# Eight retention states a head updated four at a time, on two halves of the array

## The chip, the cores and the metric

One of the eight cores of one Trainium2 chip runs the whole program: no other core takes part. The metric is the device time of one execution in microseconds (us), the median of the runs. A core has five engines that run side by side and meet at semaphores: TensorE (PE in the profile, its weight loads PEld), VectorE (DVE), ScalarE (ACT), GpSimd (POOL) and SyncE (SP). Here POOL and SP mostly issue DMAs.

## The reference

The reference is one inference step of a two-layer trunk on 336 tokens: 16 meta tokens and 256 prompt tokens, and 8 samples of 8 tokens that carry a state. Only the retention branch matters here, and in it the new states of the samples. For each layer, head and sample:

```python
def retention_chunk(S, q, k, v):
    ...
    scores = jnp.einsum('bihd,bjhd->bhij', q, k) * decay[None]
    intra = jnp.einsum('bhij,bjhe->bihe', scores, v)
    inter = jnp.einsum('bihd,bhde->bihe', q, S) * q_decay[None, :, :, None]
    S_new = S * jnp.exp(n * lg)[None, :, None, None] + jnp.einsum('bjhd,bjhe->bhde', k * k_decay[None, :, :, None], v)
    return S_new, intra + inter
```

A state S is 256 x 256 in float32. There are 2 layers, 8 heads and 8 samples, so 128 states. Each is read from memory, used for `inter`, scaled by a constant of its head, increased by a product of the sample's eight keys and values, and written back.

## The kernel before, in words

All large products run as float32r matmuls on PE, with operands split into a high and a low part (`hi_of` on ACT, `lo_of` on DVE), so that each product is three matmuls: hi by hi, hi by lo, lo by hi. The work is a list of 720 steps. One step is one weight block of 512 KB: `dma_step` loads it from SP some steps ahead (tile `raw`), `split_step` splits it two steps ahead (`whi` on ACT, `wlo` on DVE), and `main_step` issues its 24 matmuls on PE into the tile `acc`. Everything else is an event: `at(s, fn)` puts `fn` behind `main_step(s)` in program order. The order is written out by hand, and each engine works off its own instructions strictly in that order. So an event's matmuls stand in PE's queue between two steps, and PE waits there if their operands are not ready. Events of one step run in the order in which they were registered.

A head of the retention branch takes 16 steps: four each for k, v, q and the gate rg. `head(h)` (from L302) registers its events with `E(d, fn)`, d steps from the head's first. Events with d of 16 and over run during the next head. Those that matter, with their d:

- `turn` transposes k and v into tokens with DVE's 32 x 32 transposes (L333), in four parts; v's last part is at 12.
- `tok` (L159, L165) splits the 128-token blocks of k and v: the high part by ACT, the low part by DVE. Block 2 holds the samples' tokens. For v, blocks 2 and 0 are at 13 and block 1 at 14.
- `stack_out` writes block 2 of the split k or v to a scratch in DRAM from POOL (`ktd`, `vtd`), and `stack_in` reads it back from SP so that the 32 rows of a sample (eight tokens, four combinations of high and low parts) stand on 32 partitions. For k this is the tile `kts`, 128 partitions by 2 groups of four samples. For v it is `vbd`, block-diagonal: four slots of 256 columns a group, of which sample j fills only slot j on its own 32 partitions, and the rest stays zero.
- `ev_q` at 11 rotates q on DVE (four operations, L307 to L310). `split_q` at 12 makes `qhi` (ACT) and `qlo` (DVE), and copies the samples' columns to `qpad` (POOL). `scores2` at 14 multiplies them with k on PE: first khi by qhi, then khi by qlo, and so on.
- `inter` at 15 multiplies `qpad` with the states, in 32 matmuls of 32 stationary columns; `inter_copy` at 16 takes the result.
- `sdo(b)` at 17 + b updates one state: two matmuls of 128 rows by 256 columns (the rows of the other three samples meet zeros), one DVE operation over 512 columns (L444) and one DMA out from POOL (L445). `sload(b)` at 6 + b is the load of one state.
- `pstate`, the prompt's new state, is at 18; `pv` and `norm2` at 17 to 25; `back` at 26 transposes the head's result on PE (L511), and DVE takes it (L513).

In the first head of layer 0 (`kl = 3`) k's events are three steps later, and all four parts of v's `turn` are at 12. PSUM tiles of the events come from a ring of four (`side`).

Of the kernel before, what the change touches and what calls it, by code (L numbers as in the profile page):

```python
# [6 lines left out]
F32 = mybir.dt.float32  # L7
F32R = mybir.dt.float32r
ACTF = mybir.ActivationFunctionType
ALU = mybir.AluOpType  # L10
# [7 lines left out]
NB = 8  # L18
# [3 lines left out]
HD = 256  # L22
# [55 lines left out]
def build(tc, a, o, g8):  # L78
    nc = tc.nc
# [6 lines left out]
    def at(s, fn, *args):  # L86
        events[s].append(lambda: fn(*args))

    def job(wsrc, nk, rhs, c0, evac, lag=0):
        first = len(steps)  # L90
        st = dict(acc=None)
        for j in range(nk):
            steps.append((st, wsrc(j), rhs, 4 * j, c0, j == 0, j == nk - 1))
        last = first + nk - 1
        at(last + lag, lambda: evac(st["acc"]))
        return first, last

    def wblk(w, c):
        return lambda j: w[c // 256, j].rearrange("p (k n) -> p k n", k=4)
# [3 lines left out]
    def open_pool(name, side=None, **kw):  # L103
        P[name] = tc.alloc_tile_pool(name=name, bufs=1, side=side, reuse_waits="tile", **kw)
        return P[name]
# [15 lines left out]
    def side():  # L121
        return sidep.tile([128, 512], F32, tag="side", bufs=4, name="side")
# [31 lines left out]
    def mm(out, lhsT, rhs, start, stop):  # L154
        nc.tensor.matmul(out, lhsT, rhs, start=start, stop=stop)  # L155
# [105 lines left out]
    H = {}  # L261

    for l in range(DEPTH):
# [13 lines left out]
        def open_r(l=l, a_side=a_side):  # L277
            p = open_pool("r", side=a_side)
            t = p.tile([128, 2, 8, 32], F32, name="qpad")
            nc.gpsimd.memset(t, 0.0)  # L280
            H["qpad"] = t
            for key in ("kr", "vr"):
                t = p.tile([128, 2, 384], F32, name=key)
                nc.gpsimd.memset(t[:, :, T:384], 0.0)
                H[key] = t
            t = p.tile([128, SC], F32, name="sc")
            nc.gpsimd.memset(t[64:128, NR0 + NR1:SC], 0.0)
            H["sc"] = t
            t = p.tile([128, 2, 4, HD], F32R, name="vbd")
            nc.gpsimd.memset(t.bitcast(F32), 0.0)  # L290
            H["vbd"] = t
            for key in ("kt", "vt"):
                t = p.tile([128, HD], F32R, name=key + "tail")
                nc.gpsimd.memset(t[64:128].bitcast(F32), 0.0)
                H[key + "tail"] = t
# [4 lines left out]
        def head(h, l=l, c0=c0, n=n, nt=nt):  # L300
            hs = {}
            rp = lambda shape, dt, tag, bufs=1: P["r"].tile(shape, dt, tag=tag, bufs=bufs, name=tag)  # L302
# [47 lines left out]
            def stack_in(key):  # L350
                rows = hs[key + "d"].rearrange("g c t e -> (g c t) e")
                nc.sync.dma_start(out=H[key + "tail"][0:64].bitcast(F32), in_=rows[0:64])
                src = rows[64:320].rearrange("(f r) e -> r f e", f=2)
                if key == "kt":
                    st = hs["kts"] = rp([128, 2, HD], F32R, "kts")
                    nc.sync.dma_start(out=st.bitcast(F32), in_=src)
                else:
                    for j in range(4):
                        r = slice(32 * j, 32 * j + 32)
                        nc.sync.dma_start(out=H["vbd"][r, :, j].bitcast(F32), in_=src[r])  # L360

            def pstate():
                ps = side()
# [56 lines left out]
                lo_of(plo[:, w], sc[:, w], phi[:, w])  # L420
                hs["p"] = phi, plo

            def sload(b):
                s = rp([128, 2, HD], F32, "sraw", 8)
                nc.sync.dma_start(out=s, in_=a["state_ret"][l, b, h].rearrange("p (d e) -> p d e", d=2))
                hs["s", b] = s

            def inter():
                ps = hs["inter"] = side()
# [4 lines left out]
                            mm(ps[32 * j:32 * j + 32, :HD], H["qpad"][:, d, b], hs["s", b][:, d],  # L434
                               i == 0 and d == 0, i == 1 and d == 1)

            def sdo(b):
                up = side()
                for d in range(2):
                    mm(up[:, HD * d:HD * d + HD], hs["kts"][:, b // 4, 128 * d:128 * d + 128],  # L440
                       H["vbd"][:, b // 4, b % 4], True, True)
                s = hs.pop(("s", b))
                s2 = s.rearrange("p d e -> p (d e)")
                nc.vector.scalar_tensor_tensor(out=s2, in0=s2, scalar=g8[h], in1=up, op0=ALU.mult, op1=ALU.add)  # L444
                nc.gpsimd.dma_start(out=o["ret_s"][l, b, h].rearrange("p (d e) -> p d e", d=2), in_=s)  # L445

            def ev_rg(acc):
                z, th = tmp(), tmp()
# [69 lines left out]
            b0, e = job(wblk(w_in, OFF["k"] + HD * h), 4, h_rhs, 0, ev_k, 3 if l == 0 and h == 0 else 0)  # L518
# [3 lines left out]
            E = lambda d, fn, *ar: at(b0 + d, lambda: fn(*ar))  # L522
# [7 lines left out]
            E(9 + kl, tok, 0, "k", kd(0))  # L530
            E(10 + kl, tok, 1, "k", kd(1))
            E(11 + kl, stack_in, "kt")
            E(13, tok, 2, "v", None)
            E(13, stack_out, "vt")
            E(13, tok, 0, "v", None)
            E(14, tok, 1, "v", None)
            E(15, stack_in, "vt")
            E(12, split_q)
            E(18, pstate)
            E(11, scores)  # L540
            E(14, scores2)
            for b in range(NB):
                E(6 + b, sload, b)
            E(15, inter)
            for b in range(NB):
                E(17 + b, sdo, b)
            E(16, inter_copy)
            E(17, pv, 0)
            E(18, norm2, 0)
            E(19, pv, 1)  # L550
            E(20, norm2, 1)
            E(24, pv, 2)
            E(25, norm2, 2)
            E(26, back)
# [3 lines left out]
        if l == 0:  # L558
            at(6, open_r)
        else:  # L560
            at(r0 - 1, open_r)
        for h in range(HEADS):
            head(h)
# [272 lines left out]
        if l == 0:  # L836
            e = len(steps) - 1
# [87 lines left out]
    for j, (ps, (t0, rows)) in enumerate(zip(sums, YBLOCKS)):  # L925
        nc.vector.tensor_scalar(out=trs[:rows, j:j + 1], in0=ps[:rows, 0:1], scalar1=1.0 / DM, scalar2=EPS,
                                op0=ALU.mult, op1=ALU.add)
# [67 lines left out]
```

## Time and profile before

| | |
|---|---|
| Median of 3 runs (all runs) | 2817.84 us (2817.78, 2817.84, 2819.44) |
| Profiled execution: its time | 2819.04 us |
| Profiled execution: span from first to last instruction | 2816.9 us |
| PE busy | 2800.1 us (99%), 19042 matmuls |
| DVE busy | 1684.9 us (60%) |
| ACT busy | 940.2 us (33%) |
| POOL busy | 291.9 us (10%) |
| Granted PE clock, mean | 0.997 |
| DMA | 516.64 MB, mean 183 GB/s |

The span is what the profile sees; 2.1 us of the execution's time lie around it. Busy PE time is modelled: matmuls overlap one another, so the time that a matmul takes away from the others is read from the distance between two starts, not from its duration. In a timeline the columns are the start in us, the duration in us, engine, line, operation, tile written and tiles read, shape and count, and in brackets the idle time before it and what ended that. An acc row is a matmul of a step, a side row is one of an event.

### The profile page before, as it was taken

The page shows a single profiled execution, that of the slowest core. Times are in us where ns is not written, and L with a number is a line of the kernel's source. Part 1 is how long each engine was busy: PE and PEld are TensorE (multiplying, and loading weights), DVE is VectorE, ACT ScalarE, POOL GpSimd, SP SyncE. Part 2 cuts the span into 40 slices and gives each one's busy share as a digit, 9 for nine tenths or more (in the row PEclk, how much of TensorE's full clock was granted, in tenths as well). Part 3 has the DMA queues.
Part 4 walks back from the last instruction along what each step waited for, and adds up shares of the span by engine and source line. Part 5 has one row for each costly group of instructions (what it writes and reads, how often), then busy time and mean ns, then how long its engine had stood idle before and what let it go on. Part 6 is the DMA issues. An engine that isn't in the chain of part 4 may idle for free.

```text
span 2816.9 us, 46574 instructions
## 1 busy us (share of the span) xinstructions
PE 2800.1 (99%) x19042; PEld 2778.0 (99%) x19042; DVE 1684.9 (60%) x2418; ACT 940.2 (33%) x1121; POOL 291.9 (10%) x547
## 2 busy tenths in 40 slices
PE   9999999999999999999999999999999999999998
PEld 9999999999999999999999999999999999999998
DVE  8777777744345664344467777777543455644543
ACT  5333333333233333233333333333332333333333
POOL 1211111110000000000112212211100000000001
PEclk9999999999999999999999999999999999999999
DMA  6666665655544444444546666666555454444443
GB/s 228 227 211 212 212 212 207 216 200 170 166 163 149 147 148 135 155 167 163 188 167 218 219 225 225 215 213 212 207 182 173 161 166 148 145 158 164 173 163 129
DMA packets 174262, 516.64 MB, mean 183 GB/s; under 512 B 23888, under 2 KB 46672, under 8 KB 174032
## 3 DMA queue, kind: packets, MB, share of 16 engines
q1 hardware_dynamic: 151264, 448.37, 46.6%
q0 software_dynamic: 21696, 63.99, 6.4%
q8 instruction: 149, 2.44, 0.4%
q10 hardware_dynamic: 1088, 1.31, 0.1%
q14 instruction: 65, 0.53, 0.1%
HBM read 447.91 MB, written 66.57 MB: 183 GB/s over the span
## 4 chain that ended last, share of the span: by engine, by line
PE 99%; DVE 1%; DMA 0%; issue 0%; POOL 0%; SPq 0%; DVEq 0%; ACT 0%; ACTq 0%
PE acc L155 93%; PE side L155 6%; PE side L511 0%; DVE tok L333 0%; DMA raw<-in_w_in_dram 0%; DVE xf L937 0%; DVE wlo L165 0%; PE side L252 0%; POOL trs L928 0%; DVE qlo L165 0%; DVE tmp L307 0%; DVE tmp L308 0%; DVE whi L190 0%; DVEq L983 0%; DVE xs L809 0%
## 5 line engine op out<-in xcount | busy, mean ns | idle before, releaser
L155 PE MATMUL acc<-act_hi,whi 128*128 128x320 f32 (+1 forms) x3328 | 1038.0, 312 | 0.0
L155 PE MATMUL acc<-act_lo,whi 128*128 128x320 f32 (+1 forms) x3328 | 1037.5, 312 | 0.0
L155 PE MATMUL acc<-act_hi,wlo 128*128 128x320 f32 (+1 forms) x3328 | 1036.1, 311 | 0.0
L165 DVE TENSOR_TENSOR wlo<-raw,whi 128x1024 fp32r<-128x1024 f32 (+1 forms) x721 | 866.1, 1219 | 262.4 <-ACT whi L159 251.7
L159 ACT CAST whi<-raw 128x1024 fp32r<-128x1024 f32 x719 | 736.6, 1046 | 619.3 <-PE acc L155 445.6
L155 PE MATMUL acc<-h_hi,whi 128*128 128x336 f32 x2304 | 731.0, 319 | 0.0
L155 PE MATMUL acc<-h_lo,whi 128*128 128x336 f32 x2304 | 728.2, 318 | 1.1 <-DVE h_lo L167 1.1
L155 PE MATMUL acc<-h_hi,wlo 128*128 128x336 f32 x2304 | 726.2, 317 | 0.0
L155 PEld LDWEIGHTS acc<-act_hi,whi 128*128 128x128 f32 x3328 | 624.8, 188 | 3.3 <-ACT tmp L450 3.3
L155 PEld LDWEIGHTS acc<-act_lo,whi 128*128 128x128 f32 x3328 | 626.4, 188 | 0.0
L155 PEld LDWEIGHTS acc<-act_hi,wlo 128*128 128x128 f32 x3328 | 625.2, 188 | 0.0
L155 PEld LDWEIGHTS acc<-h_lo,whi 128*128 128x128 f32 x2304 | 435.8, 190 | 1.5 <-DVE h_lo L167 1.5
L155 PEld LDWEIGHTS acc<-h_hi,whi 128*128 128x128 f32 x2304 | 432.5, 188 | 3.6 <-ACT tmp L450 3.3
L155 PEld LDWEIGHTS acc<-h_hi,wlo 128*128 128x128 f32 x2304 | 433.2, 188 | 0.0
L444 DVE SCALAR_TENSOR_TENSOR sraw<-sraw,side 128x512 f32<-128x512 f32 x128 | 87.7, 685 | 185.3 <-PE side L155 185.3
L445 POOL DMA_DIRECT2D out_ret_s_dram<-sraw x128 | 70.7, 552 | 566.4 <-DVE sraw L444 560.7
L333 DVE STREAM_TRANSPOSE tok<-vr 32x192 f32<-32x192 f32 (+1 forms) x256 | 90.3, 353 | 4.3
L333 DVE STREAM_TRANSPOSE tok<-kr 32x192 f32<-32x192 f32 (+1 forms) x256 | 90.3, 353 | 4.1
L611 DVE SCALAR_TENSOR_TENSOR mb<-tr,acc 128x336 f32<-128x336 f32 (+1 forms) x32 | 14.4, 492 | 81.0 <-PE acc L155 81.0
L775 DVE SCALAR_TENSOR_TENSOR mt<-tp,acc 128x336 f32<-128x336 f32 (+1 forms) x32 | 14.4, 492 | 80.4 <-PE acc L155 80.4
L809 DVE SCALAR_TENSOR_TENSOR xs<-acc,xo 128x672 f32<-128x672 f32 (+2 forms) x17 | 13.5, 800 | 80.5 <-PE acc L155 80.5
L275 DVE TENSOR_TENSOR tp<-acc,rstd 128x672 f32<-128x672 f32 (+1 forms) x16 | 13.5, 841 | 80.4 <-PE acc L155 80.4
(170 smaller groups left out, 1756.1 us busy)
## 6 DMA issues: line engine op xcount, KB each, us to landing
raw<-in_w_in_dram SPq DMA_DIRECT2D x512, 512.0 KB, 4.3
sraw<-in_state_ret_dram SPq DMA_DIRECT2D x128, 256.0 KB, 4.7
out_ret_s_dram<-sraw POOLq DMA_DIRECT2D x128, 256.0 KB, 3.5
raw<-in_proj_ret_dram SPq DMA_DIRECT2D x64, 512.0 KB, 4.1
raw<-in_proj_pool_dram SPq DMA_DIRECT2D x64, 512.0 KB, 4.9
raw<-in_w_out_dram SPq DMA_DIRECT2D x64, 512.0 KB, 4.7
raw<-in_pool_w_dram SPq DMA_DIRECT2D x16, 512.0 KB, 3.3
kts<-ktd SPq DMA_DIRECT2D x16, 256.0 KB, 3.2
```

The source lines that it names most:

```text
L155: nc.tensor.matmul(out, lhsT, rhs, start=start, stop=stop)
L159: nc.scalar.copy(out=out, in_=in_)
L165: nc.vector.tensor_tensor(out=out, in0=in_, in1=hi.bitcast(F32), op=ALU.subtract)
L275: nc.vector.tensor_tensor(out=tile_[:, :, n], in0=acc[:, :, n], in1=bc(rstd[:, n]), op=ALU.mult)
L333: nc.vector.transpose(dst[32 * t:32 * t + 32, :, 0:nb, a_], src[q, :, 0:nb, t])
L444: nc.vector.scalar_tensor_tensor(out=s2, in0=s2, scalar=g8[h], in1=up, op0=ALU.mult, op1=ALU.add)
L445: nc.gpsimd.dma_start(out=o["ret_s"][l, b, h].rearrange("p (d e) -> p d e", d=2), in_=s)
L611: nc.vector.scalar_tensor_tensor(out=t[:, d, n], in0=H["tr", l, i][:, d, n], scalar=1.0, in1=acc[:, d, n], op0=ALU.add, op1=ALU.mult)
L775: nc.vector.scalar_tensor_tensor(out=t[:, d, n], in0=H["tp", l, i][:, d, n], scalar=1.0, in1=acc[:, d, n], op0=ALU.add, op1=ALU.mult)
L809: nc.vector.scalar_tensor_tensor(out=xs[:, p, n], in0=acc[:, p, n], scalar=0.5, in1=xo[:, p, n], op0=ALU.mult, op1=ALU.add)
```

## The change

The states are held, loaded and written in pairs. `sload(p)` loads samples 2p and 2p + 1 with one DMA, at 6 + 2p. `vbd` keeps two slots instead of four: sample j goes to slot j mod 2, so that a group's partitions 0 to 63 hold samples 0 and 1 as a block diagonal, and 64 to 127 samples 2 and 3. `update(g)` replaces four calls of `sdo`: for each half d of the state's rows and each half r of the partitions, one matmul of 64 rows by 512 columns into a PSUM tile of its own, then four DVE operations of 512 columns, then two DMAs out. The two halves r use different rows of the array and different PSUM tiles. The events are moved too: v's `tok` of block 2 and `stack_out` from 13 to 12, ahead of `split_q`; `stack_in` of v from 15 to 14; `scores2` from 14 to 13; `inter` from 15 to 14; `inter_copy` from 16 to 15; the updates from 17 to 24 to 16 and 18; `pv` 0 and 1 to 20 and 21; `pstate` from 18 to 23.

```diff
-            t = p.tile([128, 2, 4, HD], F32R, name="vbd")
+            t = p.tile([128, 2, 2, HD], F32R, name="vbd")
...
-                        nc.sync.dma_start(out=H["vbd"][r, :, j].bitcast(F32), in_=src[r])
+                        nc.sync.dma_start(out=H["vbd"][r, :, j % 2].bitcast(F32), in_=src[r])
...
-            def sload(b):
-                s = rp([128, 2, HD], F32, "sraw", 8)
-                nc.sync.dma_start(out=s, in_=a["state_ret"][l, b, h].rearrange("p (d e) -> p d e", d=2))
-                hs["s", b] = s
+            def sload(p):
+                s = rp([128, 2, 2, HD], F32, "sraw", 4)
+                nc.sync.dma_start(out=s, in_=a["state_ret"][l, 2 * p:2 * p + 2, h].rearrange("b p (d e) -> p b d e", d=2))
+                for b in range(2):
+                    hs["s", 2 * p + b] = s[:, b]
+                hs["pair", p] = s
...
-            def sdo(b):
-                up = side()
-                for d in range(2):
-                    mm(up[:, HD * d:HD * d + HD], hs["kts"][:, b // 4, 128 * d:128 * d + 128],
-                       H["vbd"][:, b // 4, b % 4], True, True)
-                s = hs.pop(("s", b))
-                s2 = s.rearrange("p d e -> p (d e)")
-                nc.vector.scalar_tensor_tensor(out=s2, in0=s2, scalar=g8[h], in1=up, op0=ALU.mult, op1=ALU.add)
-                nc.gpsimd.dma_start(out=o["ret_s"][l, b, h].rearrange("p (d e) -> p d e", d=2), in_=s)
+            def update(g):
+                ups = [(d, r, side()) for d in range(2) for r in range(2)]
+                for d, r, up in ups:
+                    rows = slice(64 * r, 64 * r + 64)
+                    mm(up, hs["kts"][rows, g, 128 * d:128 * d + 128],
+                       H["vbd"][rows, g].rearrange("p j e -> p (j e)"), True, True)
+                for d, r, up in ups:
+                    s = hs["pair", 2 * g + r]
+                    nc.vector.scalar_tensor_tensor(out=s[:, :, d], in0=s[:, :, d], scalar=g8[h],
+                                                   in1=up.rearrange("p (j e) -> p j e", j=2), op0=ALU.mult, op1=ALU.add)
+                for r in range(2):
+                    p = 2 * g + r
+                    nc.gpsimd.dma_start(out=o["ret_s"][l, 2 * p:2 * p + 2, h].rearrange("b p (d e) -> p b d e", d=2),
+                                        in_=hs["pair", p])
...
-            E(13, tok, 2, "v", None)
-            E(13, stack_out, "vt")
+            E(12, tok, 2, "v", None)
+            E(12, stack_out, "vt")
             E(13, tok, 0, "v", None)
             E(14, tok, 1, "v", None)
-            E(15, stack_in, "vt")
+            E(14, stack_in, "vt")
             E(12, split_q)
-            E(18, pstate)
             E(11, scores)
-            E(14, scores2)
-            for b in range(NB):
-                E(6 + b, sload, b)
-            E(15, inter)
-            for b in range(NB):
-                E(17 + b, sdo, b)
-            E(16, inter_copy)
-            E(17, pv, 0)
-            E(18, norm2, 0)
-            E(19, pv, 1)
-            E(20, norm2, 1)
+            E(13, scores2)
+            for p in range(4):
+                E(6 + 2 * p, sload, p)
+            E(14, inter)
+            E(15, inter_copy)
+            E(16, update, 0)
+            E(18, update, 1)
+            E(20, pv, 0)
+            E(21, norm2, 0)
+            E(21, pv, 1)
+            E(22, norm2, 1)
+            E(23, pstate)
             E(24, pv, 2)
             E(25, norm2, 2)
             E(26, back)
```

## Rows read from the trace of the kernel before

**Rows 1.** The page: busy time and share, and the chain that ended last.

```profile
PE 2800.1 (99%) x19042; PEld 2778.0 (99%) x19042; DVE 1684.9 (60%) x2418; ACT 940.2 (33%) x1121; POOL 291.9 (10%) x547
PE 99%; DVE 1%; DMA 0%; issue 0%; POOL 0%; SPq 0%; DVEq 0%; ACT 0%; ACTq 0%
```

**Rows 2.** The page's costliest groups: count | busy us, mean ns of one | idle before.

```profile
L444 DVE SCALAR_TENSOR_TENSOR sraw<-sraw,side 128x512 f32<-128x512 f32 x128 | 87.7, 685 | 185.3 <-PE side L155 185.3
L445 POOL DMA_DIRECT2D out_ret_s_dram<-sraw x128 | 70.7, 552 | 566.4 <-DVE sraw L444 560.7
```

**Rows 3.** Timeline of PE: two states' updates and what starts behind each.

```profile
302.80 0.40 PE L155 MATMUL side<-vbd,kts 128*128 128x256 f32 x2
303.03 0.28 PE L155 MATMUL side<-vthi,phi 128*128 128x256 f32 x1
...
307.45 0.40 PE L155 MATMUL side<-vbd,kts 128*128 128x256 f32 x2
307.69 0.32 PE L155 MATMUL acc<-h_hi,whi 128*128 128x336 f32 x1
```

**Rows 4.** Timeline of PE around one inter; its second row is of a shorter stretch.

```profile
353.13 0.31 PE L155 MATMUL acc<-h_hi,wlo 128*128 128x336 f32 x1
353.37 0.42 PE L155 MATMUL side<-sraw,qpad 128*32 128x256 f32 x4
353.37 1.93 PE L155 MATMUL side<-sraw,qpad 128*32 128x256 f32 x32
355.23 0.42 PE L155 MATMUL acc<-h_hi,whi 128*128 128x336 f32 x1
355.49 0.31 PE L155 MATMUL acc<-h_lo,whi 128*128 128x336 f32 x1
```

**Rows 5.** Timeline of DVE in the fifth head of layer 0.

```profile
332.71 1.04 DVE L513 SCALAR_TENSOR_TENSOR tmp<-side,vec,sg 128x336 f32<-128x336 f32 x2 [0.46 <-PE side L511]
343.66 0.86 DVE L165 TENSOR_TENSOR qlo<-tmp,qhi 128x672 fp32r<-128x672 f32 x1
```

**Rows 6.** Timeline of ACT in the same head.

```profile
339.41 0.76 ACT L159 CAST qhi<-tmp 128x672 fp32r<-128x672 f32 x1 [6.06 <-DVE tmp L310]
343.32 0.74 ACT L159 CAST vthi<-tok 80x256 fp32r<-80x256 f32 x2 [2.21 <-DVE tok L333]
```

**Rows 7.** Timeline of PE in the same head: first matmuls of step 14 and of scores2.

```profile
343.99 0.32 PE L155 MATMUL acc<-h_hi,whi 128*128 128x336 f32 x1
347.71 0.29 PE L155 MATMUL side<-qhi,khi 128*128 128x272 f32 x1
```

**Rows 8.** Timeline of DVE in the second head of layer 1.

```profile
1543.48 1.01 DVE L513 SCALAR_TENSOR_TENSOR tmp<-side,vec,sg 128x320 f32<-128x320 f32 x2
1554.29 0.83 DVE L165 TENSOR_TENSOR qlo<-tmp,qhi 128x640 fp32r<-128x640 f32 x1
```

**Rows 9.** Timeline of ACT in the second head of layer 1.

```profile
1553.96 0.75 ACT L159 CAST vthi<-tok 80x256 fp32r<-80x256 f32 x2 [2.23 <-DVE tok L333]
```

**Rows 10.** Timeline of PE there: first matmuls of step 14 and of scores2.

```profile
1554.13 0.31 PE L155 MATMUL acc<-act_hi,whi 128*128 128x320 f32 x1
1557.63 0.28 PE L155 MATMUL side<-qhi,khi 128*128 128x256 f32 x1
```

**Rows 11.** Timeline of PE in the first head of layer 0: scores2.

```profile
64.75 0.29 PE L155 MATMUL side<-qhi,khi 128*128 128x272 f32 x1
66.64 0.39 PE L155 MATMUL side<-qlo,khi 128*128 128x272 f32 x1 [1.60 <-DVE qlo L165]
```

**Rows 12.** Timelines of ACT and DVE in that head.

```profile
64.60 0.74 ACT L159 CAST vthi<-tok 80x256 fp32r<-80x256 f32 x2 [4.12 <-DVE tok L333]
64.93 0.88 DVE L167 SCALAR_TENSOR_TENSOR ktlo<-tok,cst,kthi 80x256 fp32r<-80x256 f32 x2
65.73 0.85 DVE L165 TENSOR_TENSOR qlo<-tmp,qhi 128x672 fp32r<-128x672 f32 x1
```

**Rows 13.** Busy time by stretch: engines' us, then the granted clock, DMA share, GB/s.

```profile
67.90:71.20 3.30, 3.30 (x17) 3.30 (x16) 3.00 (x7) 0.26 (x1) 3.30 (x5) 0.50 0.27 66
```

## The prediction

> **What bounds the kernel now.** I read the page first. PE is busy for 99% of the span, and the chain that ended last is 99% PE [rows 1]. So what counts is PE's time: matmuls that are taken off it are worth what they occupy, and a wait that the change puts into PE's queue costs its full length. DVE, ACT, POOL, SP and the DMAs cost something only where PE comes to wait for them. Next I read the timelines of PE around the updates, for what they occupy, and around `inter`, the one place where this kernel already splits the array. Last I read DVE, ACT and PE together from `back` to `scores2`, because the change moves `scores2` one step forward.
>
> **What the updates occupy now.** There are 128 states, each with one operation on L444 and one DMA on L445 [rows 2], and two matmuls for each. What a pair takes from PE is the distance of starts: 302.80 to 303.03 and 307.45 to 307.69, 0.23 and 0.24 us, so some 0.118 a matmul [rows 3]. The updates occupy 256 x 0.118 = 30.2 us. The change makes 32 batches, each in place of eight matmuls, 0.94 us.
>
> **What they will occupy.** A matmul of 512 columns should take twice one of 256, 0.236 us. If the two halves stream at once, a batch streams for 2 x 0.236 = 0.47 us; if they don't, for 4 x 0.236 = 0.94. No row shows matmuls of 64 rows. The nearest is `inter`, which splits the array by columns: four of its matmuls start within 0.04 us of one another, and 32 of them take 353.37 to 355.23, 0.058 us each, half of what a full-array matmul of as many columns takes, though each is a slower f32 pass [rows 3, 4]. So parts of the array do work at once here, and I take the halves to do so.
>
> The same rows price the passage from whole array to parts and back. A step's matmuls follow each other in 3.72 / 24 = 0.155 us [rows 7]. The last one ahead of `inter` is followed after 0.24 (0.085 too much). From there to the next step's first matmul it is 1.86 us; the groups of four follow each other in (1.93 - 0.42) / 7 = 0.216, eight of them are 1.73, and the other 0.13 is passage; and the first matmul behind it occupies 0.26, 0.105 too much, because its weights could not be loaded ahead [rows 4]. Together 0.32 us [rows 4]. A half of the array gets 128 columns of weights where `inter` gets 32; I add 0.08 for that, from the 0.105 that 128 exposed columns cost, and take 0.40 a batch. So a batch is 0.47 + 0.40 = 0.87 us and 32 are 27.9: **2 us gained**. With no price for the passage it is 15.1 us and the gain 15.1; with the passage and no overlap it is 32 x 1.34 = 42.9 us and a loss of 13. I take the 2, since the passage of `inter` is the nearest row, and keep both ends.
>
> The Trainium skill has this as a rule against the change: by its page TensorEngine Tiling (Array Packing), Key Properties, a switch of the tiling mode drains the array. The 0.32 us around `inter` agree for columns; no row shows it for halves of rows. By the rule the gain is the 2 us, without it the 15.
>
> **The step that decides: scores2 one step earlier.** DVE's line from `back` to `qlo` is fixed. At `back` DVE waits for PE (0.46 us idle ahead of L513), and from there to `qlo` it has no idle time worth a row: 332.71 to 343.66 [rows 5]. In layer 1 the same line runs from 1543.48 to 1554.29 [rows 8]. None of the work that the change takes off DVE lies in these steps (`back` is d = 10, `qlo` d = 12 of the next head; the evacuations were at d = 1 to 8 and will be at 0 and 2). The line's start is tied to PE's transposes, so a lighter DVE before that doesn't pull it forward.
>
> PE reaches `scores2` now at 347.71, one step behind 343.99 [rows 7]; it will reach it at 343.99, and its second matmul, the one that reads `qlo`, would be due at 344.12. Now `qlo` ends at 344.52 [rows 5]: already 0.4 late. And the change puts v's `tok` of block 2 ahead of `split_q` in step 12. On ACT the high part of v, which waits for v's last transposes until 343.32, now stands in front of `qhi`, which today ran at 339.41 [rows 6]. So `qhi` starts at 343.32 + 0.34 (two such casts take 0.74) = 343.66 and ends 0.76 later at 344.42; `qlo` needs it, takes 0.86 and ends at 345.30; PE sees that 0.05 later (66.58 to 66.64 in the first head [rows 11, 12]), at 345.35. **The wait is 345.35 - 344.12 = 1.23 us**, in seven heads of layer 0. In layer 1: v's high part at 1553.96, `qhi` (0.73, as 640 of 672 columns of 0.76) 1554.30 to 1555.03, `qlo` to 1555.88, PE at 1555.93, due at 1554.13 + 0.13 = 1554.26: **1.67 us**, in eight heads [rows 8 to 10].
>
> In the first head of layer 0 PE waits already, 1.76 us from 64.88 to 66.64 [rows 11]. There all of v's transposes are in step 12, and v's low part (0.40, as one of the two ktlo) now stands ahead of `qlo`: 65.73 + 0.40 + 0.85 + 0.05 = 67.03 [rows 12]. PE is due at 64.75 - 3.72 + 0.13 = 61.16. The wait becomes 5.87 us, 4.1 more.
>
> Sum: 7 x 1.23 + 8 x 1.67 + 4.1 = **26.1 us lost**. The lower bound has `qhi` untouched and `qlo` later by v's low part alone (0.40): 0.85 and 1.31 us a head, 7 x 0.85 + 8 x 1.31 + 4.1 = 20.5. I take 26.1: the order in ACT's queue is plain in the diff.
>
> **The clock.** Behind the 1.76 us wait of the first head the granted clock was 0.50 from 67.90 to 71.20 [rows 13], the lower of the two levels (1.2 of 2.4 GHz): half of 3.3 us, some 1.65 us, were lost again. The new waits are 1.23 and 1.67 us, with one matmul in between; whether they cost the clock too no row says. I count none beyond the first head's, which has its loss already; the other end is 15 x 1.65 = 25 us.
>
> **Edits that I cost at nothing.** DVE's evacuations: the same number, 8 of 0.69 us a head [rows 2], over as many elements, now in two bursts of 2.7 us behind steps 16 and 18, where DVE has one split of weights a step and little else; if that cover failed, `wlo` of two steps later would be late by what is over. The four PSUM tiles of a batch: the last of them is `inter`'s, which `inter_copy` must have read. It comes behind the gate's work: one operation of 672 columns on DVE (as `qlo`, 0.86), one on ACT (as `qhi`, 0.76), two of 336 on DVE (as L513, 1.04), then the copy's low part (as ktlo, 0.4), 3.1 us in all [rows 5, 6, 12]. The batch starts a step behind the gate's last matmul, 3.5 to 3.7 us, its fourth matmul later still. If the copy were late, that matmul alone would wait, some tenths. The states' loads: the same bytes, pair 3 issued at 12 and read at 14, now with PE's wait in between. v's way through DRAM: each link one step earlier, the distances between them as now; but `qpad`'s copies on POOL now queue behind four DMA issues, two of which wait for v's low part (343.7 + 0.4). With 0.55 us an issue [rows 2] the copies begin near 346; PE reads `qpad` in `inter`, a step behind `scores2`, past 349. `pv`, `norm2` and `pstate` move in the queue and occupy what they did; k's and v's tiles are written again only at d = 9 to 14 of the next head. 64 fewer DMA issues each on SP and POOL relieve queues that bound nothing.
>
> **The sum.** 26.1 - 2.3 (30.2 - 27.9) = 23.8 us more. The profiled execution took 2819.04 us, 2816.9 of them span; it would take 2842.8. The median of the runs is 1.2 lower: 2817.84 + 23.8 = **2841.6 us**.
>
> **The rivals.**
> - *The halves cost no passage.* For it: `inter`'s cost could be that of column parts. The gain is 15.1: 2817.84 + 26.1 - 15.1 = 2828.8. Chance 0.17.
> - *The clock falls at the waits.* For it: the first head's 1.76 us did it; against: the others are shorter. If all eight of layer 1 do, 8 x 1.65 = 13 us: 2855; if all 15, 2866. Chance 0.14.
> - *The halves stream one after the other.* For it: no row shows rows split. 42.9 - 30.2 + 26.1 = 38.8: 2856.6. Chance 0.06.
> - *Faster after all: the batches stream freely and the waits are short.* The place is DVE's line from L513 to `qlo`. Were it shorter by some 0.7 us a head, because it starts earlier than PE's transposes let it now or ACT takes `qhi` first, the waits would fall below 15.1 us in all, 0.94 a head; that is the point from which it decides. With waits of 8 us: 2817.84 - 15.1 + 8 = 2811. For it: layer 1's L513 shows no idle time in its row; against: the line needs 10.8 us and has three steps, 10.5 to 11.2. Chance 0.14; another 0.07 lies around no change, with waits of 11 to 20 us.
>
> **How the numbers follow.** The forecast, 2841.6, has 0.42; with the unknowns of its own terms 2833 to 2850. For 8 in 10 the range takes in the free passage with the lower wait (2817.84 + 20.5 - 15.1 = 2823), most of what lies around no change and, above, the serial halves and the clock falling in most heads: **2818 to 2864**. A measurement of this kernel tells 0.2%, 5.6 us, from no change. Faster: 0.14. Within 0.2% (2812.2 to 2823.5): 0.07. Slower, the forecast and the first three rivals: 0.79.
>
> **What would show it.** Right: PE rows of `scores2` with an idle time ended by DVE `qlo` in all 16 heads, 0.7 to 1.7 us each, and 5 to 6 us in the first; ACT's `qhi` directly behind the first `vthi`; two vbd matmuls of 512 columns that start together, 0.8 to 0.9 us from the step's last matmul to where the next would have been. Wrong: no idle time at `scores2`, or pairs of vbd matmuls 0.24 us apart.

## The result, and the profile after

The changed kernel takes 2847.1 us (median; 2845.75 to 2848.62), the kernel before, on the same chip, 2818.4: a ratio of 1.0101 with a 95% interval of 1.0089 to 1.0113. It is 28.7 us slower; the forecast was 23.8 slower, at 2841.6. The profiled execution has a span of 2845.5 us, 28.6 more than before. The page now shows PE on 92% of the chain that ended last, where it was 99% [rows 1], with DVE in between:

```profile
span 2845.5 us, 45976 instructions
PE 2809.9 (99%) x18914; PEld 2761.7 (97%) x18914; DVE 1685.7 (59%) x2418; ACT 936.6 (33%) x1121; POOL 277.3 (10%) x483
PE 92%; DVE 5%; issue 1%; ACT 0%; DMA 0%; POOL 0%; SPq 0%; DVEq 0%; ACTq 0%
L447 DVE SCALAR_TENSOR_TENSOR sraw<-sraw,side 128x512 f32<-128x512 f32 x128 | 79.3, 682 | 56.1 <-PE side L155 56.1
L451 POOL DMA_DIRECT2D out_ret_s_dram<-sraw x64 | 46.2, 726 | 362.7 <-DVE sraw L447 344.7
```

DVE does the same 128 operations of 0.68 us and POOL half as many DMA issues [rows 2]. PE's busy share says little: a step's matmul is given 0.31 us where the next could follow after 0.155, so a part of each wait counts as busy. The view of who waited for whom tells it. For PE its first two rows (us in total, times, longest) are these:

```profile
PE side L155 <- ACT qhi L159: 12.1, 16, 4.5
PE side L155 <- DVE qlo L165: 8.0, 16, 0.7
```

Sixteen heads, sixteen waits for each: all at `scores2`. Before there was one, of 1.6 us [rows 11]. In the timelines of the fifth head of layer 0 the line from `back` to `qlo` is the one of [rows 5 to 7], but for v's split, which now stands ahead of q's on ACT (`vthi` ahead of `qhi`) and on DVE (`vtlo` ahead of `qlo`). PE with one weight load, then ACT, then DVE:

```profile
353.09 0.31 PE L155 MATMUL acc<-h_hi,wlo 128*128 128x336 f32 x1
353.68 0.39 PE L155 MATMUL side<-qhi,khi 128*128 128x272 f32 x1 [0.27 <-ACT qhi L159]
354.57 0.39 PE L155 MATMUL side<-qlo,khi 128*128 128x272 f32 x1 [0.50 <-DVE qlo L165]
354.80 0.29 PE L155 MATMUL side<-qhi,klo 128*128 128x272 f32 x1
...
354.57 0.19 PEld L155 LDWEIGHTS side<-qlo,khi 128*128 128x128 f32 x1 [0.71 <-DVE qlo L165]
...
352.56 0.41 ACT L159 CAST vthi<-tok 80x256 fp32r<-80x256 f32 x1 [9.95 <-DVE tok L333]
352.88 0.75 ACT L159 CAST qhi<-tmp 128x672 fp32r<-128x672 f32 x1
...
341.96 1.04 DVE L520 SCALAR_TENSOR_TENSOR tmp<-side,vec,sg 128x336 f32<-128x336 f32 x2 [0.46 <-PE side L518]
...
348.13 0.50 DVE L310 TENSOR_TENSOR tmp<-tmp 128x336 f32<-128x336 f32 x1
...
351.39 1.48 DVE L333 STREAM_TRANSPOSE tok<-vr 32x192 f32<-32x192 f32 x4
353.00 0.42 DVE L165 TENSOR_TENSOR vtlo<-tok,vthi 80x256 fp32r<-80x256 f32 x1
353.65 0.86 DVE L165 TENSOR_TENSOR qlo<-tmp,qhi 128x672 fp32r<-128x672 f32 x1 [0.23 <-ACT qhi L159]
```

ACT now stands idle for 9.95 us, until v's last transposes are done; for the last 3.9 of them `qhi`, behind the instruction that waits, could have run, since its operand is done at 348.63 (L310). From 353.09 the first matmul of `scores2` would start 0.155 later; it starts after 0.59. The second should follow after 0.125 and follows after 0.89. The third still comes 0.105 late: the second's weights were loaded only with it, both at 354.57, and not ahead of it. Together 0.435 + 0.765 + 0.105 = 1.3 us. In layer 1:

```profile
1569.12 0.30 PE L155 MATMUL acc<-act_hi,wlo 128*128 128x320 f32 x1
1570.15 0.38 PE L155 MATMUL side<-qhi,khi 128*128 128x256 f32 x1 [0.74 <-ACT qhi L159]
1571.01 0.39 PE L155 MATMUL side<-qlo,khi 128*128 128x256 f32 x1 [0.47 <-DVE qlo L165]
1571.23 0.28 PE L155 MATMUL side<-qhi,klo 128*128 128x256 f32 x1
```

That is 0.88 + 0.74 + 0.10 = 1.73 us (1.5 in the first head of layer 1, which has no `back` ahead of it). In the first head of layer 0:

```profile
60.95 0.31 PE L155 MATMUL acc<-h_hi,wlo 128*128 128x336 f32 x1
65.78 0.59 PE L155 MATMUL side<-qhi,khi 128*128 128x272 f32 x1 [4.52 <-ACT qhi L159]
67.04 0.59 PE L155 MATMUL side<-qlo,khi 128*128 128x272 f32 x1 [0.67 <-DVE qlo L165]
```

4.68 + 1.13 = 5.8 us, 4.05 more than the 1.76 before. A batch of the new updates:

```profile
227.46 0.31 PE L155 MATMUL acc<-h_hi,wlo 128*128 128x336 f32 x1
227.70 0.73 PE L155 MATMUL side<-vbd,kts 64*128 64x512 f32 x4
228.36 0.42 PE L155 MATMUL acc<-h_hi,whi 128*128 128x336 f32 x1
228.62 0.32 PE L155 MATMUL acc<-h_lo,whi 128*128 128x336 f32 x1
```

From 227.46 to 228.62 it is 1.16 us, of which two ordinary distances are 0.31: a batch takes 0.85, where eight matmuls took 0.94. And the granted clock, by stretch:

```profile
64.70:74.80 10.10, 8.35 (x34) 8.05 (x35) 7.47 (x14) 5.49 (x9) 4.00 (x10) 0.50 0.40 114
1921.50:1924.80 3.30, 3.30 (x14) 3.30 (x14) 2.35 (x4) 2.57 (x4) 0.07 (x1) 0.50 0.07 24
1925.00:1928.00 3.00, 3.00 (x39) 2.23 (x41) 1.50 (x3) 0.02 (x1) 0.00 (x0) 1.00 0.57 149
```

It is 0.50 over 10.1 us in the first head, where before it was so over 3.3 [rows 13], and once more behind one of the 15 other waits, that of the seventh head of layer 1. PE worked from 67.04 to 74.8 of the first stretch, so 3.9 us were lost there (1.65 before), and 1.65 in the second: 3.9 more than before.

The account: waits 7 x 1.3 + 1.5 + 7 x 1.73 + 4.05 = 26.8; clock 3.9; batches 32 x (0.85 - 0.94) = -2.9. Sum 27.8 of 28.6 us. Compared step by step, by the distances between the first matmuls of the 720 steps, all of the difference lies in the two retention stages, 13.6 and 14.3 us, and none in the stages behind them; 0.7 us of the span lies ahead of the first step and behind the last.

### The profile page after: what moved, and what is told of

Its sections match the earlier page's. It is cut to its first block, busy times and chain, and to the rows that moved or that the text cites. A ratio compares the mean times of both kernels' runs of the same rounds, so it can differ in the third digit from the quotient of the medians.

```text
span 2845.5 us, 45976 instructions
## 1 busy us (share of the span) xinstructions
PE 2809.9 (99%) x18914; PEld 2761.7 (97%) x18914; DVE 1685.7 (59%) x2418; ACT 936.6 (33%) x1121; POOL 277.3 (10%) x483
## 4 chain that ended last, share of the span: by engine, by line
PE 92%; DVE 5%; issue 1%; ACT 0%; DMA 0%; POOL 0%; SPq 0%; DVEq 0%; ACTq 0%
PE acc L155 87%; PE side L155 5%; DVE tok L333 2%; DVE wlo L165 1%; DVE tmp L520 1%; DVE qlo L165 0%; DVE tmp L307 0%; DVE tmp L308 0%; ACT qhi L159 0%; DVE tmp L310 0%; DVE ktlo L167 0%; PE side L518 0%; DMA raw<-in_w_in_dram 0%; DVE xf L944 0%; PE side L252 0%
## 5 line engine op out<-in xcount | busy, mean ns | idle before, releaser
L447 DVE SCALAR_TENSOR_TENSOR sraw<-sraw,side 128x512 f32<-128x512 f32 x128 | 79.3, 682 | 56.1 <-PE side L155 56.1
L451 POOL DMA_DIRECT2D out_ret_s_dram<-sraw x64 | 46.2, 726 | 362.7 <-DVE sraw L447 344.7
L159 ACT CAST vthi<-tok 128x256 fp32r<-128x256 f32 (+1 forms) x48 | 19.3, 403 | 153.1 <-DVE tok L333 153.1
```

The source lines that it names most:

```text
L159: nc.scalar.copy(out=out, in_=in_)
L447: nc.vector.scalar_tensor_tensor(out=s[:, :, d], in0=s[:, :, d], scalar=g8[h], in1=up.rearrange("p (j e) -> p j e", j=2), op0=ALU.mult, op ...
L451: nc.gpsimd.dma_start(out=o["ret_s"][l, 2 * p:2 * p + 2, h].rearrange("b p (d e) -> p b d e", d=2), in_=hs["pair", p])
```

## The experiments

The theory at this point: the loss is PE's wait at `scores2`, because `scores2` came one step forward and `qhi` went behind v's high part in ACT's queue; the batches alone are a small gain. Its rival: the batches, their passage and DVE's bursts are what costs. All ratios are to the kernel before, timed in the same series.

**Moving scores2 back alone** (a_scores14, from the changed kernel).

```diff
-            E(13, scores2)
+            E(14, scores2)
```

> The changed kernel with one event moved back: scores2 at 14 instead of 13. Theory (the loss is PE's wait at scores2 for qlo): the wait is gone in 15 heads; the first head of layer 0 keeps one of about 2.2 us (1.8 before, v's low part of 0.4 now ahead of qlo). The batches keep their gain of 3.1 us, as the trace of the changed kernel has it (a batch 0.85 us, eight matmuls before 0.94). 2818.4 - 3.1 + 0.4 = 2815.7 us. Rival (the batches and DVE's bursts are what costs): the time stays at 2845 to 2847.

Measured: 2818.1 us, ratio 1.000 (0.9991 to 1.0010). So 29.0 us, the whole loss, hang on that step, and the rival falls. It is 2.4 us above the theory's number, and the trace shows both parts. In the first head `inter` now stands directly behind `scores2`, and `qpad`'s copies on POOL, behind the DMA issues of v's scratch, are late:

```profile
70.01 3.64 PE L155 MATMUL side<-sraw,qpad 128*32 128x256 f32 x32 [0.82 <-POOL qpad L393]
67.70:74.40 6.70, 5.88 (x45) 3.55 (x45) 4.73 (x8) 2.05 (x4) 2.66 (x6) 0.50 0.51 144
```

0.8 us of wait, and the clock at half for 6.7 us instead of 3.3: another 1.7.

**Putting split_q ahead of v's split** (b_qfirst, from the changed kernel), with `scores2` still at 13: what belongs to v's split, now ahead of q's, and what to DVE's line?

```diff
+            E(12, split_q)
             E(12, tok, 2, "v", None)
...
-            E(12, split_q)
```

> The changed kernel with split_q registered ahead of v's tok of block 2 in step 12, so that qhi no longer queues behind v's high part on ACT; scores2 stays at 13. Theory: the wait shrinks to what DVE's line alone gives, 0.45 us in seven heads, 0.91 in eight, about 5.4 in the first, each with some 0.13 behind it for the weight load that could not be pulled ahead: 16 us more than before, 3.1 less for the batches, 2 for the clock in the first head: about 2833 us. Rival (DVE's line alone makes the wait, ACT's order is no matter): unchanged, 2847. Rival (ACT's order alone): 2818 or less.

Measured: 2834.8 us, ratio 1.0057 (1.0042 to 1.0072), against 2833 expected. The order of the two splits is worth 12.4 of the 28.7 us; the other 16.4, net of the batches' gain, are DVE's line, which isn't done in time even with `qhi` early. PE's waits are now for `qlo` alone, and none for `qhi`; in the fifth head the second matmul follows the first after 0.59 instead of 0.125, a wait of 0.46 (0.45 expected):

```profile
PE side L155 <- DVE qlo L165: 13.3, 16, 5.3
...
351.42 0.29 PE L155 MATMUL side<-qhi,khi 128*128 128x272 f32 x1
352.01 0.39 PE L155 MATMUL side<-qlo,khi 128*128 128x272 f32 x1 [0.30 <-DVE qlo L165]
```

The 12.4 us are not ACT's queue alone, as the expectation puts it. The edit also takes v's low part from ahead of `qlo` on DVE. In the changed kernel's fifth head it is 0.78 us from the end of v's last transposes (352.87) to the start of `qlo` (353.65); v's low part takes 0.42 of that, and the wait for `qhi` behind it only 0.23. So with ACT's order alone put right, some 0.23 us a head would come back, an estimate from these rows; no run parts the two.

**Putting split_q ahead of v's transposes too** (c_qtop, from the changed kernel): the event is registered before the loop that registers `turn`.

```diff
             E(4 + kl, split_k)
+            E(12, split_q)
...
-            E(12, split_q)
```

> The changed kernel with split_q registered first of all in step 12, ahead of v's last transposes too (ahead of all four parts of them in the first head); scores2 stays at 13. Theory: qlo ends some 1.5 us earlier than in the kernel before and is there when PE comes, in all heads, the first too: no wait at scores2 and no fall of the clock behind it. 2818.4 - 3.1 (batches) - 1.9 (the first head's wait) - 1.7 (its clock) = 2811.7 us. Rival (scores2 at 13 is too early whatever stands ahead of it, or the batches cost): 2820 to 2847.

Measured: 2813.6 us, ratio 0.9984 (0.9974 to 0.9993): faster than both kernels, by 4.7 us against the one before. No row of PE's waits names qhi or qlo, and in the same head `qlo` is done at 338.87 where PE needs it at 340.10 (DVE, then PE):

```profile
338.02 0.85 DVE L165 TENSOR_TENSOR qlo<-tmp,qhi 128x672 fp32r<-128x672 f32 x1
338.90 1.48 DVE L333 STREAM_TRANSPOSE tok<-vr 32x192 f32<-32x192 f32 x4
...
339.97 0.29 PE L155 MATMUL side<-qhi,khi 128*128 128x272 f32 x1
340.10 0.28 PE L155 MATMUL side<-qlo,khi 128*128 128x272 f32 x1
```

So 13 is not too early for `scores2` as such; what stood ahead of `qlo` made it so. It is 1.9 us above the expected time. Step by step, the first head gives 3.3 us (its wait and its clock; the whole stretch from 57 to 70 us has a granted clock of 1.00), the batches 1.4 in layer 0 and 0.9 in layer 1, less than 3.1.

```profile
57.00:70.00 13.00, 13.00 (x111) 11.86 (x110) 12.01 (x29) 3.69 (x8) 4.76 (x8) 1.00 0.15 42
```

**The order alone, without halves and pairs** (d_order_only). The kernel before with its own loads, tiles and matmuls, and the changed kernel's events:

```diff
-            E(13, tok, 2, "v", None)
+            E(12, tok, 2, "v", None)
...
-            E(14, scores2)
+            E(13, scores2)
...
-                E(6 + b, sload, b)
+                E(6 + b // 2 * 2, sload, b)
...
-                E(17 + b, sdo, b)
+                E(16 + b // 4 * 2, sdo, b)
```

> The kernel before, with its loads, its vbd of four slots and its matmuls of 128 rows by 256 columns, in the changed kernel's order of events: four calls of sdo at 16 and four at 18, two loads of a state at 6, 8, 10 and 12. Theory: all of the loss and none of the batches' gain: 2847.1 + 3.1 = 2850 us. Rival (the halves of the array or the pairs are what costs): 2818 us.

Measured: 2849.7 us, ratio 1.0109 (1.0094 to 1.0124). The whole loss is there without a single matmul on a half. PE's two rows of waits are those of the changed kernel, to the digit: 12.1 us for qhi and 8.0 for qlo. The clock fell behind two of the 15 shorter waits here (at 1573 and 1645 us).

What the halves themselves are worth was then measured on c_qtop, which has no wait at `scores2`, in a second series on another chip; the kernel before takes 2818.3 us in both.

**Each batch's matmuls twice** (f_twice; the second time writes the same values again).

```diff
-                for d, r, up in ups:
+                for d, r, up in ups + ups:
                     rows = slice(64 * r, 64 * r + 64)
```

> c_qtop with the four matmuls of every batch issued twice (the second time writes the same values). It prices the streaming of a pair of halves apart from the passage. Theory (halves stream at once, a pair takes 512 columns at 2.4 GHz and little more; 0.85 us a batch is two pairs and some 0.42 of passage): 32 x 2 x 0.216 = 13.8 us more than c_qtop, 2827.4 us. Rival (no passage, a pair simply takes 0.33 us, its distance in the changed kernel's trace): 32 x 2 x 0.33 = 21 us more, 2834.7.

Measured: 2828.3 us, ratio 1.0035 (1.0022 to 1.0049); 14.7 more than c_qtop, 0.46 a batch, 0.23 a pair of halves.

```profile
358.56 0.31 PE L155 MATMUL acc<-h_hi,wlo 128*128 128x336 f32 x1
358.80 1.20 PE L155 MATMUL side<-vbd,kts 64*128 64x512 f32 x8
359.92 0.42 PE L155 MATMUL acc<-h_hi,whi 128*128 128x336 f32 x1
360.18 0.31 PE L155 MATMUL acc<-h_lo,whi 128*128 128x336 f32 x1
```

358.56 to 360.18 is 1.62 us, 0.46 more than the 1.16 of four matmuls. So two halves of 512 columns do stream at once, in 0.23 us, and the other 0.85 - 0.46 = 0.39 us of a batch is the passage from the whole array to halves and back.

**The batch on the whole array** (g_whole): 128 rows by 512 columns, four slots in `vbd`.

```diff
-                    rows = slice(64 * r, 64 * r + 64)
-                    mm(up, hs["kts"][rows, g, 128 * d:128 * d + 128],
-                       H["vbd"][rows, g].rearrange("p j e -> p (j e)"), True, True)
+                    mm(up, hs["kts"][:, g, 128 * d:128 * d + 128],
+                       H["vbd"][:, g, 2 * r:2 * r + 2].rearrange("p j e -> p (j e)"), True, True)
```

> c_qtop with the batch's four matmuls on the whole array: 128 rows by 512 columns, vbd with four slots again, nothing else changed. Theory (four whole matmuls stream 4 x 0.22 to 0.236 us without a passage, against 0.85 of the batch): 0.03 to 0.09 us more a batch, 1 to 3 us more than c_qtop: 2815 to 2816.5. Rival (halves are worth the half of 30 us): 2827.

Measured: 2815.3 us, ratio 0.9988 (0.9979 to 0.9997); 1.7 above c_qtop.

```profile
355.27 0.31 PE L155 MATMUL acc<-h_hi,wlo 128*128 128x336 f32 x1
355.43 1.09 PE L155 MATMUL side<-vbd,kts 128*128 128x512 f32 x4
356.35 0.32 PE L155 MATMUL acc<-h_hi,whi 128*128 128x336 f32 x1
```

Here the batch begins 0.16 behind the last matmul and the next follows 0.92 after its start: no passage, but four streams of 0.23. Halves save half of the streaming, 0.46 us a batch, and the passage takes 0.39 of it back.

**The halves one after the other in program order** (h_halfwise).

```diff
-                ups = [(d, r, side()) for d in range(2) for r in range(2)]
+                ups = [(d, r, side()) for r in range(2) for d in range(2)]
```

> c_qtop with a batch's matmuls in the other order: both of the first half, then both of the second, with DVE's operations in that order too. Theory (only neighbours in PE's queue can run at once, so just the two in the middle overlap: three streams of 0.213 instead of two): 32 x 0.21 = 6.8 us more, 2820.4. Rival (the halves run independently of the order): as c_qtop, 2813.6.

Measured: 2814.0 us, ratio 0.9982 (0.9973 to 0.9991): as c_qtop. The expectation was wrong.

```profile
354.83 0.31 PE L155 MATMUL acc<-h_hi,wlo 128*128 128x336 f32 x1
355.07 0.50 PE L155 MATMUL side<-vbd,kts 64*128 64x512 f32 x2
355.07 0.74 PE L155 MATMUL side<-vbd,kts 64*128 64x512 f32 x4
355.73 0.42 PE L155 MATMUL acc<-h_hi,whi 128*128 128x336 f32 x1
```

The second row is of a stretch that ends at 355.08: two matmuls have started by then, although the first two in the program are on the same half. All four take the time of two streams and the passage, 0.66 us from first start to the next step. Three streams would have taken 0.2 more. So one half's matmul must have started ahead of an earlier one that waits for the other half; which of the four stands in which row the trace doesn't say. That each engine works off its instructions strictly in order, as said of the kernel before, does not hold here.

**One line in the kernel before** (i_before_qtop): `split_q` first in step 12, nothing else.

```diff
             E(4 + kl, split_k)
+            E(12, split_q)
...
-            E(12, split_q)
```

> The kernel before with one line moved: split_q first of all in step 12. No halves, no pairs, scores2 stays at 14. Theory: it takes away the first head's wait (1.9 us with the weight load behind it) and its fall of the clock (1.6 us) and nothing else: 2818.3 - 3.5 = 2814.8 us; so c_qtop (2813.6) owes 3.5 of its gain to this line and 1 to 2.4 to the batches. Rival (c_qtop's gain is the batches'): 2818.

Measured: 2816.9 us, ratio 0.9994 (0.9985 to 1.0003): not clear of no change, and 2.1 above the expected time. The first head's wait at `scores2` and its fall of the clock are gone, but part of that comes back one step later, where PE now waits for a split of weights that v's sixteen transposes hold up on DVE:

```profile
66.42 0.32 PE L155 MATMUL acc<-h_lo,whi 128*128 128x336 f32 x1
67.46 0.42 PE L155 MATMUL acc<-h_hi,wlo 128*128 128x336 f32 x1 [0.72 <-DVE wlo L165]
...
66.19 1.22 DVE L165 TENSOR_TENSOR wlo<-raw,whi 128x1024 fp32r<-128x1024 f32 x1
```

By the medians this line gives 1.5 of c_qtop's 4.7 us; by the spans of the profiled executions 2.4 of 5.2, all of it in the first head. The rest belongs to the batches together with the earlier order, which no run parts.

## Why the prediction was right, point by point

- **What bounds it.** Right: the difference is matmuls and waits in PE's queue, and nothing in the stages without them.
- **scores2.** Right, and by the mechanism named: the wait without the matmul behind it was forecast at 1.23, 1.67 and 5.87 us, and is 1.20, 1.62 and 5.8. In layer 0 DVE's line starts from PE's transposes with 0.46 us of idle time, as before, however light DVE's steps ahead of it became. b_qfirst parts what the order of the splits adds from what DVE's line alone gives, a_scores14 and d_order_only show that it is the whole loss. Two things came out otherwise than written. The sign named one wait, for `qlo`; there are two, and the larger in total is for `qhi` (12.1 us against 8.0), which the first matmul of `scores2` reads; the end of the second is as forecast. And less of the wait is ACT's than the choice of 26.1 over the lower bound makes it: that bound has `qlo` behind v's low part alone, and behind that part DVE waited only 0.23 us for `qhi` in the fifth head.
- **The batch.** Right: 0.87 forecast, 0.85 measured, with 0.39 of passage (0.40 forecast) and 0.23 for a pair of halves (0.236). The rule of the Trainium skill (TensorEngine Tiling (Array Packing), Key Properties), that a change of tiling mode drains the array, agrees with the 0.39 us here. The rivals without a passage (2828.8) and with halves one after the other (2856.6) are out.
- **The clock.** The term that was mis-sized: none was counted beyond the first head's 1.65 us. It is 3.9 in the first head, whose wait grew to 5.8 us, and 1.65 behind one of the other 15: 3.9 more than before. The rival "in all heads" is out: one of 15 here, two of 15 in d_order_only.
- **What was left out.** The matmul behind a wait costs 0.1 us more, since its weights could not be loaded ahead: 1.6 us in 15 heads. The clock and this are, nearly, the 5.5 us between 2841.6 and 2847.1.
- **Edits at nothing.** No wait of PE names the update's PSUM tiles, the states' loads, v's scratch or `qpad` in the changed kernel. `qpad` was closer than I had it: in a_scores14, with `inter` directly behind `scores2`, it was late by 0.8 us in the first head. The batch's last PSUM tile was close too: in c_qtop the fourth matmul of the first head's first batch starts 0.33 us behind the third, and the next step follows the batch's start after 1.06 us instead of 0.66.

## What to carry to other kernels

When an event moves one step forward in a hand-written order, follow each of its operands back to the engine that makes it, and count what the same edit puts ahead of that in the engine's queue: here v's split, which waits for data, came to stand ahead of q's in two queues, and that cost 12.4 of the 28.7 us; the rest went because the operations that make `qlo` were not done a step earlier even without it. Halves of the array are worth it only for batches long against the passage (0.39 us in and out here, against 0.46 of streaming saved). A loss that sits beside a gain in one edit can be parted from it by one line, and the repaired version beat both.

## What was unexpected in the hardware

Matmuls on different halves of the array need not alternate in the program: with both of one half first, two matmuls still started within 0.01 us of each other, and the batch took the time of the alternating order, not the 0.2 us more that a third stream would have taken. A wait of 1.2 to 1.7 us on PE mostly left the granted clock at its higher level (27 times of 30 in the two kernels that have 15 such waits each), while 1.76 us in the first head, before, and 5.8 us, after, cost stretches of 3.3 and 10.1 us at the lower one.
